# Hybrid encoder layer: one settle a round for VectorE's search tiles, all gates ahead of attention, low parts of the attention keys and values on GpSimd

## The chip, the core and the metric

The kernel runs on one core of a Trainium2 chip. The time is that of one execution on the device, in microseconds; a run gives one such time. Several engines work side by side, each through its own instructions in the order in which they were written to its queue: TensorE (PE; its weight loads are listed as PEld), VectorE (DVE), ScalarE (ACT), GpSimd (POOL) and SyncE (SP), which issues the DMA transfers.

## What is computed

One encoder layer over T = 1088 tokens (1024 of the prompt, 64 of a sample) with 1024 features: half a SwiGLU step, then a mixer, then half a SwiGLU step. Cut to the mixer, which the change touches:

```python
u = _rms(h, mix_norm)
q, k, v, qi, ki, wi, conv_in, gate = jnp.split(u @ w_in, points, axis=-1)   # after rotary: q, k, qi, ki
# sparse attention: each query keeps the top 256 admissible keys by an indexer score
score = jnp.einsum('bqh,bqhs->bqs', wi, jax.nn.relu(jnp.einsum('bqhd,bsd->bqhs', qi, k_idx)))
_, sel = lax.top_k(jnp.where(admissible, score, -jnp.inf), top)
attn = softmax(q . k[sel] / 8) @ v[sel]                                       # 8 heads, 2 key/value heads
# convolution branch
dc = depthwise_conv(concat(past_conv, ca * sigmoid(cb)), conv_w) + conv_b     # 31 taps, 512 channels
conv_out = silu(_layernorm(dc)) @ conv_w_out
# merge
g_a, g_c = split(sigmoid(gate + b_gate))                                      # 2 x 1024 gate columns
h = h + (g_a * (attn @ attn_w_out) + g_c * conv_out) @ w_out
```

## The kernel before

Values are kept transposed, features on the 128 partitions and tokens along the row. Tokens go in three chunks (`CHUNKS`) of 362 to 364. A float32 product is made of three matmuls on high and low parts (`mm3`, L136 to L138): high times high, high times low, low times high. A high part is a rounded copy that ScalarE makes, a low part the difference, a subtraction on VectorE or GpSimd (`split`, L152 and L153; for weights `wload`: DMA into `raw` at L117, `whi` on ScalarE at L118, `wlo` on GpSimd at L119).

The program around the change runs in these stages, of the profiled execution's 2411.5 us: the first SwiGLU to about 760 us, then the input projections and the indexer's scores, and then, from about 1060 us on, several kinds of work side by side:

- **The search** for the 256th best score of each query. Seven query tiles (named 5, 4, 3, 2, 1, 0, 6, with 1024, 896, 768, 640, 512, 384 and 192 keys) are searched by halving: each score is cut into a high and a low half of 16 bits; 15 rounds on the high halves (`search(15, …)`), `low_half` to prepare the low ones, 16 rounds on the low halves (`search(16, …)`). One round of one tile is a count of the keys at or above the candidate threshold (`count`; L907 on VectorE, L904 on ScalarE) and a settling, which moves the candidate up or down: on VectorE three small instructions for a group of tiles at once (`settle`, L914, L916, L918), on ScalarE two for each tile (`settle_x`, L925, L926). ScalarE has tile 5 in the 15-bit half and tiles 5 and 4 in the 16-bit half; VectorE has the rest in two groups, and the second group's counts stand between the first group's settling instructions.
- **The masks** (L964 to L984) that VectorE makes of the thresholds when the search is over, six instructions per tile, `bias` being the result.
- **The gates** (`gates`): 16 blocks of 128 gate columns, each 72 matmuls (three chunks of 24), evicted by ScalarE's tanh (`sg`, L1005) and stored to DRAM (`d_g`, L1006). `GPRE` = 14 blocks run ahead of attention, the last two as the first steps of the background.
- **The convolution**: for 60 rounds ScalarE makes `pd` (L679) and GpSimd adds it (L680).
- **The keys and values for attention** (`K`, `vt`), loaded and split while the search runs.

Then **attention** over nine query tiles in the order `TORD`, four pairs of heads each. `soft` makes a pair's logits (`lg`, matmuls L1052 and L1053) and VectorE adds the mask and takes the maximum (`pr`, `mb`, L1055); then ScalarE's exponential; `turn` transposes the probabilities (`pt`, L1079) and splits them into `ph` and `pl`; `values` multiplies them with `vt` into `pv`, which is evicted to `oh` and stored to `d_at`. Three pairs of logits run ahead of the pair that is being turned. After each slot of a pair, `fill` takes FILL[tile] steps of a **background** generator: the last gates, layer norm of the convolution (`norm`; `lx` loaded, `ls` added at L1141), its output product (`conv_out`), and for a chunk whose tiles are done `merge` (the stored attention is read back as `ar`, split into `ah` and `al`, multiplied, and gated by `ga`) and `wout`. After attention come the last merge and the second SwiGLU.

The order within each engine's queue comes from a scheduling of the whole program when it is built, in which the search and the masks have a high priority (`THI`); on the chip each engine keeps that order. The memory of the layer norm's pool (`ln`) is free only when the gates have read the activations `u`.

## Time and profile before

| | |
|---|---|
| median of 3 runs | 2418.17 us (2414.04 to 2422.6) |
| the profiled execution | 2413.27 us, its span 2411.5 us |
| mean granted TensorE clock | 0.987 |
| busy: PE, DVE, ACT, POOL | 96%, 73%, 50%, 58% of the span |
| DMA | 273.47 MB, 113 GB/s on average |

The span is what the profiler saw from the first to the last instruction. The busy share is an average over all stages; the change touches the stretch from about 1060 us to 1660 us, where the engines' shares are different from it. The granted clock is the share of full speed that TensorE was given, 1.0 being 2.4 GHz and 0.5 being 1.2 GHz.

### The profile page before, as it was taken

The numbers are of one execution on the slowest core, as the hardware profiler recorded it, in microseconds if no ns is written. First come the engines' busy times: TensorE is split into PE (matmuls) and PEld (weight loads), VectorE is DVE, ScalarE is ACT, GpSimd is POOL, SyncE is SP. The second block draws the span as 40 slices with busy tenths as digits, with TensorE's granted clock in tenths as the row PEclk, the third lists the DMA queues.
The fourth block names the chain that finished last, engine by engine and source line by source line (L and its number), as shares of the span: only waits on it lengthen the run. The fifth ranks groups of instructions, "written<-read, shape, count | busy, mean of one in ns | idle before, by whom it ended". The sixth has DMA issues, their size and how long they took to land. (4 is left out here: it accounts for less than half of the span.)

```text
span 2411.5 us, 44609 instructions
## 1 busy us (share of the span) xinstructions
PE 2307.2 (96%) x16762; PEld 2274.9 (94%) x16762; DVE 1762.6 (73%) x4051; ACT 1208.3 (50%) x2365; POOL 1407.7 (58%) x866
## 2 busy tenths in 40 slices
PE   7999999999999999999978999899999999999998
PEld 6999999999999999999977889799999999999997
DVE  7766667666677387799998976758666668776666
ACT  6433445343446556867956555536434445334343
POOL 5455556555557786878733456448555556545554
PEclk9999999999999999999989999899999999999999
DMA  5332223222224334333222546563223322332223
GB/s 191 106 106 88 95 99 125 88 97 97 97 97 139 132 125 127 95 102 105 92 83 83 167 145 191 164 211 117 86 88 104 99 99 71 116 105 96 96 102 112
DMA packets 130409, 273.47 MB, mean 113 GB/s; under 512 B 17936, under 2 KB 77200, under 8 KB 130192
## 3 DMA queue, kind: packets, MB, share of 16 engines
q1 hardware_dynamic: 130192, 270.61, 33.7%
q8 instruction: 132, 2.16, 0.4%
q14 instruction: 85, 0.70, 0.1%
HBM read 231.87 MB, written 38.75 MB: 112 GB/s over the span
## 5 line engine op out<-in xcount | busy, mean ns | idle before, releaser
L119 POOL TENSOR_TENSOR wlo<-raw,whi 128x1024 fp32r<-128x1024 f32 (+1 forms) x187 | 438.0, 2347 | 372.0 <-ACT whi L118 368.2
L136 PE MATMUL ps<-x,wp 128*128 128x272 f32 x1760 | 506.3, 289 | 2.7 <-ACT wp L152 2.6
L138 PE MATMUL ps<-x,wp 128*128 128x272 f32 x1760 | 503.5, 290 | 1.6 <-DVE wp L153 1.0
L137 PE MATMUL ps<-x,wp 128*128 128x272 f32 x1760 | 505.0, 288 | 0.0
L136 PE MATMUL ps<-x,whi 128*128 128x272 f32 (+2 forms) x1544 | 482.9, 313 | 14.0 <-ACT sg L1005 7.3
L138 PE MATMUL ps<-x,wlo 128*128 128x272 f32 (+2 forms) x1544 | 481.3, 312 | 0.3 <-POOL wlo L119 0.3
L137 PE MATMUL ps<-x,whi 128*128 128x272 f32 (+2 forms) x1334 | 411.6, 309 | 0.9 <-POOL x L153 0.9
L136 PE MATMUL ps<-gh,whi 128*128 128x272 f32 x1408 | 400.1, 289 | 5.6 <-DVE spare L284 3.5
L137 PE MATMUL ps<-gl,whi 128*128 128x272 f32 x1408 | 405.2, 289 | 0.0
L138 PE MATMUL ps<-gh,wlo 128*128 128x272 f32 x1408 | 404.1, 289 | 0.0
L153 POOL TENSOR_TENSOR wlo<-raw,whi 128x1024 fp32r<-128x1024 f32 x88 | 220.1, 2502 | 260.4 <-ACT whi L152 252.7
L136 PEld LDWEIGHTS ps<-x,wp 128*128 128x128 f32 x1760 | 331.2, 188 | 3.5 <-ACT wp L152 3.5
L138 PEld LDWEIGHTS ps<-x,wp 128*128 128x128 f32 x1760 | 328.8, 188 | 3.3 <-DVE wp L153 2.7
L137 PEld LDWEIGHTS ps<-x,wp 128*128 128x128 f32 x1760 | 331.5, 188 | 0.0
L153 POOL TENSOR_TENSOR wp<-s,wp 128x512 fp32r<-128x512 f32 x176 | 255.9, 1454 | 100.5 <-ACT wp L152 100.5
L136 PEld LDWEIGHTS ps<-x,whi 128*128 128x128 f32 x1544 | 293.2, 190 | 16.9 <-ACT sg L1005 8.2
L428 DVE SCALAR_TENSOR_TENSOR h<-ps,h 128x272 f32<-128x272 f32 x384 | 164.7, 439 | 186.8 <-PE ps L138 186.1
L118 ACT ACTIVATE whi<-raw 128x1024 fp32r<-128x1024 f32 (+1 forms) x187 | 190.6, 1020 | 214.9 <-PE ps L137 105.1
L138 PEld LDWEIGHTS ps<-x,wlo 128*128 128x128 f32 x1544 | 292.8, 190 | 1.7 <-POOL wlo L119 0.6
L680 POOL TENSOR_TENSOR ac<-ac,pd 128x559 f32<-128x559 f32 x180 | 260.5, 1447 | 57.7 <-ACT pd L679 24.1
L136 PEld LDWEIGHTS ps<-gh,whi 128*128 128x128 f32 x1408 | 263.6, 189 | 6.9 <-DVE spare L284 4.0
L138 PEld LDWEIGHTS ps<-gh,wlo 128*128 128x128 f32 x1408 | 266.3, 189 | 0.0
(235 smaller groups left out, 5010.6 us busy)
## 6 DMA issues: line engine op xcount, KB each, us to landing
raw<-wf SPq DMA_DIRECT2D x337, 512.0 KB, 3.3
raw<-wf SPq DMA_DIRECT2D x32, 384.0 KB, 3.0
d_g<-sg SPq DMA_DIRECT2D x32, 181.0 KB, 1.9
d_h<-h SPq DMA_DIRECT2D x2, 2176.0 KB, 10.5
y<-t SPq DMA_DIRECT2D x32, 136.0 KB, 1.9
raw<-d_q SPq DMA_DIRECT2D x32, 128.0 KB, 3.0
raw<-d_qi SPq DMA_DIRECT2D x24, 128.0 KB, 3.0
d_g<-sg SPq DMA_DIRECT2D x16, 182.0 KB, 3.2
```

The costliest lines, as they stand in the source:

```text
L118: nc.scalar.activation(hi[:, :n], raw[:, :n], AF.Copy)
L119: self.weng.tensor_tensor(lo[:, :n], raw[:, :n], hi[:, :n], op=ALU.subtract)
L136: t.matmul(out, wh, xh, start=first, stop=False)
L137: t.matmul(out, wh, xl, start=False, stop=False)
L138: t.matmul(out, wl, xh, start=False, stop=last)
L153: (eng or nc.vector).tensor_tensor(lo, x, hi, op=ALU.subtract)
L428: nc.vector.scalar_tensor_tensor(x, p, 0.5, x, op0=ALU.mult, op1=ALU.add)
L680: nc.gpsimd.tensor_tensor(ac, ac, pd, op=ALU.add)
```

## The change

1. **Search.** VectorE's tiles are one group (`VT`): all counts of a round, then one settling of all (its first instruction stands behind the first count). In the 16-bit half ScalarE has tiles 5 and 2 in place of 5 and 4 (1024 and 640 keys in place of 1024 and 896), so VectorE counts tile 4 in every round and tile 2 only in the 15-bit half. The low results of VectorE's tiles lie in the PSUM tile `srch`, those of ScalarE's in `lobx`; the masks are made for VectorE's tiles first.
2. **Gates.** All 16 run ahead of attention, and the background begins with the layer norm.
3. **Low parts.** The low parts of the attention keys (`kl`, twice) and values (`vt`, twice) are subtracted on GpSimd in place of VectorE.
4. **Order of attention tiles.** Tile 6 comes before tile 7.

```diff
-TORD = (7, 6, 8, 5, 4, 3, 2, 1, 0)
+TORD = (6, 7, 8, 5, 4, 3, 2, 1, 0)
-GPRE = 14
...
-            def load_k(pool, r0, name, tmp=None):
+            def load_k(pool, r0, name, tmp=None, eng=None):
...
-                self.split(kh, kl, raw)
+                self.split(kh, kl, raw, eng)
...
-            COL = {n: c for c, n in enumerate((5, 4, 3, 1, 2, 0, 6))}
-            GROUPS = {15: ((5,), (4, 3, 1), (2, 0, 6)), 16: ((5, 4), (3, 1), (2, 0, 6))}
-
+            COL = {n: c for c, n in enumerate((5, 2, 4, 3, 1, 0, 6))}
+            SPLIT = {15: ((5,), (2, 4, 3, 1, 0, 6)), 16: ((5, 2), (4, 3, 1, 0, 6))}
...
-            thr, low_ = sb_[:, 0:NT], sb_[:, 16:16 + NT]
+            thr, low_, lob = (sb_[:, 16 * i:16 * i + NT] for i in range(3))
...
                 for b in range(bits - 1, -1, -1):
+                    half = 0.5 * (1 << b)
                     if next(xs, 0) is None and bits == 15:
                         low_half(XT)
-                    for n in GA:
+                    for i, n in enumerate(VT):
                         count(n, b)
-                        next(sb, None)
-                    for _ in sb:
-                        pass
-                    sa = settle(GA, b)
-                    for n in GB:
-                        count(n, b)
-                        next(sa)
-                    sb = settle(GB, b)
-                for _ in sb:
-                    pass
+                        if i == 0:
+                            nc.vector.tensor_scalar(low_[:, g], cand[:, g], -half, None, op0=ALU.add)
+                    nc.vector.tensor_tensor(flag[:, g], cnt[:, g], thr[:, g], op=ALU.is_ge)
+                    nc.vector.scalar_tensor_tensor((res if b == 0 else cand)[:, g], flag[:, g], 2 * half, low_[:, g],
+                                                   op0=ALU.mult, op1=ALU.add)
...
-            search(15, I16, hib)
-            for g in ((4,), (3, 1), (2, 0, 6)):
+            search(15, I16, hib, hib)
+            for g in ((2,), (4, 3, 1, 0, 6)):
                 low_half(g)
-            search(16, U16, lob)
-            for g in map(cols, GROUPS[16]):
+            search(16, U16, lob, lobx)
+            for lo, g in ((lob, cols(SPLIT[16][1])), (lobx, cols(SPLIT[16][0]))):
...
-            K = [load_k(ak, 32 + 32 * g, str(g)) for g in range(2)]
+            K = [load_k(ak, 32 + 32 * g, str(g), eng=nc.gpsimd) for g in range(2)]
...
-            self.split(vt[:, 0, 0:9, :], vt[:, 1, 0:9, :], raw[:, 0:9, :])
-            self.split(vt[:SMP, 0, 9, :], vt[:SMP, 1, 9, :], raw[:SMP, 9, :])
+            self.split(vt[:, 0, 0:9, :], vt[:, 1, 0:9, :], raw[:, 0:9, :], nc.gpsimd)
+            self.split(vt[:SMP, 0, 9, :], vt[:SMP, 1, 9, :], raw[:SMP, 9, :], nc.gpsimd)
...
-            run(gates(gorder[:GPRE], ep))
+            run(gates(gorder, ep))
...
-                yield from gates(gorder[GPRE:], ak)
```

The lines of the kernel after are some 18 smaller: the logits are L1034 and L1035 there (L1052 and L1053 before), the maximum L1037 (L1055), the norm's add L1123 (L1141), the three matmuls L135 to L137.

TensorE's order between the gates and the first transposes, before: three pairs of logits, and then the gate matmuls of the last two blocks (`ps<-x`), the first row being the last of the fourteenth block.

```order
L138 MATMUL ps<-x,wlo 128x362
L1052 MATMUL lg<-kh_13639,qt 128x512
L1053 MATMUL lg<-kl_13640,qt 128x512
L1052 MATMUL lg<-kh_13639,qt 128x512
L1053 MATMUL lg<-kl_13640,qt 128x512
L1052 MATMUL lg<-kh_13639,qt 128x512
L1053 MATMUL lg<-kl_13640,qt 128x512
L136 MATMUL ps<-x,whi 128x364
L137 MATMUL ps<-x,whi 128x364
L138 MATMUL ps<-x,wlo 128x364
```

The same place after, the first two rows being the end of the sixteenth block.

```order
L136 MATMUL ps<-u,whi 128x362
L137 MATMUL ps<-x,wlo 128x362
L1034 MATMUL lg<-kh_13538,qt 128x448
L1035 MATMUL lg<-kl_13539,qt 128x448
L1034 MATMUL lg<-kh_13538,qt 128x448
L1035 MATMUL lg<-kl_13539,qt 128x448
L1034 MATMUL lg<-kh_13538,qt 128x448
L1035 MATMUL lg<-kl_13539,qt 128x448
L165 MATMUL ps<-ones,ls 128x128 x8
L1034 MATMUL lg<-kh_13538,qt 128x448
```

The 144 matmuls of the last two blocks moved from behind the first logits to ahead of them, and the norm's first column sums (`ps<-ones,ls`) stand where gate matmuls stood.

VectorE's order at the end of the masks, before: the last two masks, then the first maxima.

```order
L984 SCALAR_TENSOR_TENSOR bias<-bias,H_11249 128x1024
L984 SCALAR_TENSOR_TENSOR bias<-bias,H_11249 128x896
L1055 ISA pr,mb<-lg,bias 128x512
L1055 ISA mb 128x1
L1055 ISA pr,mb<-lg,bias 128x512
L1055 ISA mb 128x1
```

The same place after.

```order
L966 SCALAR_TENSOR_TENSOR bias<-bias,H_11249 128x1024
L966 SCALAR_TENSOR_TENSOR bias<-bias,H_11249 128x640
L1123 TENSOR_TENSOR ls<-lx 128x784
L1037 ISA pr,mb<-lg,bias 128x448
L1037 ISA mb 128x1
L1037 ISA pr,mb<-lg,bias 128x448
L1037 ISA mb 128x1
```

The norm's add moved ahead of the first maximum; before, it stood behind twelve of them.

TensorE's order where the first merge begins, before: its `ah` and `al` products come in one piece, behind the values (`pv`) of the first pair of tile 4.

```order
L136 MATMUL pv<-ph,vt 64x256
L137 MATMUL pv<-pl,vt 64x256
L138 MATMUL pv<-ph,vt 64x256
L136 MATMUL ps<-ah,whi 128x362
L137 MATMUL ps<-al,whi 128x362
L138 MATMUL ps<-ah,wlo 128x362
```

After, from the third pair of tile 5 on:

```order
L1034 MATMUL lg<-kh_13538,qt 128x320
L1035 MATMUL lg<-kl_13539,qt 128x320
L135 MATMUL ps<-ah,whi 128x362 x2
L1034 MATMUL lg<-kh_13538,qt 128x320
L1035 MATMUL lg<-kl_13539,qt 128x320
L1034 MATMUL lg<-kh_13538,qt 128x320
L1035 MATMUL lg<-kl_13539,qt 128x320
L135 MATMUL pv<-ph,vt 64x256
```

The merge's matmuls moved forward by one tile and stand singly between the logits and values of that tile's pairs, each behind the return of a piece of the attention that was stored shortly before.

## Rows read from the trace of the kernel before

**Rows 1.** The page: the chain that ended last, share of the span by engine.
```profile
PE 38%; DVE 6%; DMA 2%; ACT 1%; issue 1%; POOL 0%; SPq 0%; DVEq 0%; ACTq 0%; POOLq 0%
```
**Rows 2.** Windows: length, then busy us of PE, PEld, DVE, ACT, POOL; PEclk, DMA share, GB/s.
```profile
1130.00:1140.00 10.00, 10.00 (x62) 10.00 (x61) 9.72 (x37) 6.56 (x13) 9.68 (x7) 1.00 0.34 111
...
1260.00:1270.00 10.00, 2.30 (x6) 2.02 (x7) 9.73 (x15) 1.51 (x2) 0.00 (x0) 0.50 0.05 19
```
**Rows 3.** Timeline of PE: start us, us, operation, [idle before, releaser].
```profile
1147.78 0.43 PE L136 MATMUL ps<-x,whi 128*128 128x362 f32 x1 [3.58 <-ACT sg L1005]
...
1164.31 0.43 PE L136 MATMUL ps<-x,whi 128*128 128x362 f32 x1 [2.80 <-ACT sg L1005]
...
1172.33 0.33 PE L136 MATMUL ps<-x,whi 128*128 128x362 f32 x1
...
1184.22 0.33 PE L136 MATMUL ps<-x,whi 128*128 128x362 f32 x1
...
1233.18 0.79 PE L1052 MATMUL lg<-kh,qt 128*128 128x512 f32 x1 [5.25 <-ACT sg L1005]
...
1267.70 0.79 PE L1052 MATMUL lg<-kh,qt 128*128 128x512 f32 x1 [12.28 <-DVE mb L1055]
```
**Rows 4.** Timeline of ACT in the search's 16-bit half.
```profile
1145.38 1.15 ACT L904 ACTIVATE bias<-H,cand 128x1024 bf16<-128x1024 uint16 x1 [7.44 <-DVE cand L888]
...
1160.89 1.04 ACT L904 ACTIVATE bias<-H,cand 128x896 bf16<-128x896 uint16 x1 [4.40 <-DVE srch L887]
...
1236.99 0.29 ACT L926 ACTIVATE lob<-flag,cand 128x1 f32<-128x1 f32 x1
```
**Rows 5.** Timeline of DVE in the search: end of one round, and late in the 16-bit half.
```profile
1129.30 1.15 DVE L907 TENSOR_SCALAR_CACHE_REDUCE bias<-H,cand 128x896 bf16<-128x896 int16 x1
...
1134.15 0.14 DVE L916 TENSOR_TENSOR flag<-cnt,srch 128x3 f32<-128x3 f32 x1
...
1134.52 1.15 DVE L907 TENSOR_SCALAR_CACHE_REDUCE bias<-H,cand 128x896 bf16<-128x896 int16 x1
...
1225.45 0.88 DVE L907 TENSOR_SCALAR_CACHE_REDUCE bias<-H,cand 128x640 bf16<-128x640 uint16 x1
...
1232.09 0.16 DVE L918 SCALAR_TENSOR_TENSOR lob<-flag,srch 128x3 f32<-128x3 f32 x1
```
**Rows 6.** Timeline of DVE: low parts of keys and values.
```profile
1068.55 1.41 DVE L153 TENSOR_TENSOR kl<-raw,kh 128x1216 fp32r<-128x1216 f32 x1
...
1088.61 1.36 DVE L153 TENSOR_TENSOR vt<-raw,vt 128x1152 fp32r<-128x1152 f32 x1
```
**Rows 7.** Timeline of DVE: casts in the masks, and the first maximum.
```profile
1235.32 0.16 DVE L966 CAST mi<-lob 128x3 int32<-128x3 f32 x1
...
1251.79 2.37 DVE L966 CAST mi<-lob 128x2 int32<-128x2 f32 x1
...
1266.94 0.69 DVE L1055 CUSTOM_DVE_ANT_0 pr<-lg,bias 128x512 f32<-128x512 f32 x1 [0.24 <-issue]
```
**Rows 8.** Chain of waits: start us, us, engine and operation, at the norm.
```profile
1278.07 5.02 DMA lx<-d_dc
1283.11 0.98 DVE ls L1141
```
**Rows 9.** Timeline of POOL: low parts of weights.
```profile
1249.80 4.34 POOL L119 TENSOR_TENSOR wlo<-raw,whi 128x1024 fp32r<-128x1024 f32 x1 [14.68 <-ACT whi L118]
...
1280.18 2.40 POOL L119 TENSOR_TENSOR wlo<-raw,whi 128x1024 fp32r<-128x1024 f32 x1
```
**Rows 10.** Chain of waits: the return of a piece of attention to the merge.
```profile
1417.96 2.05 DMA d_at<-oh
1420.07 2.46 DMA ar<-d_at
1422.55 0.52 ACT ah L152
1423.09 2.63 DVE al L153
```

More of the change, by code (lines that the diff above doesn't have):

```diff
@@ L757, in run @@
             hib = kp.tile([P, NT], F32, name="hib")
-            lob = kp.tile([P, NT], F32, name="lob")
+            lobx = kp.tile([P, NT], F32, name="lobx")
             flag = kp.tile([P, NT], F32, name="flag")
@@ L888, in low_half @@
                 nc.vector.memset(cand[:, cg], float(1 << 15) - 0.5)
-                if g[0] in GROUPS[16][0]:
+                if g[0] in SPLIT[16][0]:
                     start_x(cg)
@@ L893, in start_x, with search @@
                 nc.vector.scalar_tensor_tensor(thx[:, cg], thr[:, cg], 2.0, lkx[:, cg], op0=ALU.mult, op1=ALU.add)
-            def search(bits, dt, res):
-                XT, GA, GB = GROUPS[bits]
+            def search(bits, dt, res, resx):
+                XT, VT = SPLIT[bits]
+                g = cols(VT)
                 def count(n, b):
@@ L908, in count @@
                                                 accum_out=cnt[:rows, c:c + 1])
-                def settle(t, b):
-                    g = cols(t)
-                    half = 0.5 * (1 << b)
-                    nc.vector.tensor_scalar(low_[:, g], cand[:, g], -half, None, op0=ALU.add)
-                    yield
-                    nc.vector.tensor_tensor(flag[:, g], cnt[:, g], thr[:, g], op=ALU.is_ge)
-                    yield
-                    nc.vector.scalar_tensor_tensor((res if b == 0 else cand)[:, g], flag[:, g], 2 * half, low_[:, g],
-                                                   op0=ALU.mult, op1=ALU.add)
-                    yield
                 def settle_x(n, b):
@@ L925, in settle_x @@
                     nc.scalar.activation(flag[:, c], cnt[:, c], AF.Sign, bias=thx[:, c])
-                    nc.scalar.activation((res if b == 0 else cand)[:, c], flag[:, c], AF.Identity,
+                    nc.scalar.activation((resx if b == 0 else cand)[:, c], flag[:, c], AF.Identity,
                                          bias=cand[:, c], scale=-0.5 * (1 << b))
@@ L936, in xrounds @@
                     yield
-                sb = iter(())
                 xs = xrounds()
@@ L942, in search @@
                 for b in range(bits - 1, -1, -1):
+                    half = 0.5 * (1 << b)
                     if next(xs, 0) is None and bits == 15:
                         low_half(XT)
-                    for n in GA:
+                    for i, n in enumerate(VT):
                         count(n, b)
-                        next(sb, None)
-                    for _ in sb:
-                        pass
-                    sa = settle(GA, b)
-                    for n in GB:
-                        count(n, b)
-                        next(sa)
-                    sb = settle(GB, b)
-                for _ in sb:
-                    pass
+                        if i == 0:
[3 more added lines that the diff above has]
+                                                   op0=ALU.mult, op1=ALU.add)
             nc.vector.memset(cand, float(1 << 14) - 0.5)
-            start_x(cols(GROUPS[15][0]))
-            search(15, I16, hib)
-            for g in ((4,), (3, 1), (2, 0, 6)):
+            start_x(cols(SPLIT[15][0]))
+            search(15, I16, hib, hib)
+            for g in ((2,), (4, 3, 1, 0, 6)):
                 low_half(g)
-            search(16, U16, lob)
-            for g in map(cols, GROUPS[16]):
+            search(16, U16, lob, lobx)
+            for lo, g in ((lob, cols(SPLIT[16][1])), (lobx, cols(SPLIT[16][0]))):
                 nc.vector.tensor_copy(mi[:, 0, g], hib[:, g])
-                nc.vector.tensor_copy(mi[:, 1, g], lob[:, g])
+                nc.vector.tensor_copy(mi[:, 1, g], lo[:, g])
                 nc.vector.tensor_scalar(mi[:, 0, g], mi[:, 0, g], 16, None, op0=ALU.logical_shift_left)
```

## The prediction

> **What bounds the kernel now.** I read the page's chain first: TensorE carries 38% of the span on it by its own matmuls and VectorE 6%, the other engines 2% or less each [rows 1]. So an edit gains only where TensorE stands idle. The windows between 1060 and 1660 us, where all edits lie, show where that is: at 1130 to 1140 TensorE is busy for the whole window, at 1260 to 1270 for 2.30 of 10 us while VectorE is busy for 9.73 [rows 2]. TensorE's timeline gives the waits. The longest is 12.28 us before 1267.70, a logit matmul that needs its PSUM buffer back from the first maximum, and VectorE reaches that maximum only at 1266.94, when the last mask is done [rows 3, 7]. One of 5.25 us ends at 1233.18, where the first logits wait for ScalarE's last gate eviction, and two of 3.58 and 2.80 us stand among the gates for the same reason [rows 3]. ScalarE itself stood still for 7.44 and 4.40 us just ahead of these two, until VectorE had prepared the low halves of its tiles [rows 4]. VectorE is thus the head of the queue at both places: search, masks, first maximum.
>
> **Search.** A settling's last two instructions take from 1134.15 to 1134.52, that is 0.37 us in which VectorE counts nothing, and they follow a count's sum at once [rows 5]. The first instruction of the three runs under a count and is not charged. Two settlings a round become one: 31 rounds × 0.37 = 11.5 us less. Against that VectorE now counts tile 4 (896 keys, 1.15 us) where it counted tile 2 (640 keys, 0.88) in 16 rounds [rows 5]: 16 × 0.27 = 4.3 us more. That the settling of all tiles now stands directly ahead of a count which needs its result could add a latency that the order before hid. The flag, which needs the sum just made, comes without a gap [rows 5], so I take nothing for it; 31 × 0.1 = 3 us is the upper bound I keep, a quarter of the settling itself. ScalarE's second tile shrinks by as much as VectorE's grows, so ScalarE keeps to its pace; its last result came at 1236.99, and it is needed only when VectorE's five masks are done [rows 4]. Before, the masks of ScalarE's tiles began at 1251.79 [rows 7].
>
> **Low parts.** The keys' two subtractions cost VectorE 1.41 us each and the values' 1.36 [rows 6]: 4.2 us less while the search runs (the small fourth is left out). GpSimd takes them instead. For 1024 elements it needs 2.40 us [rows 9], so for 1216, 1216 and 1152 some 2.85 + 2.85 + 2.70, and about 0.4 for the small one: 8.8 us between its additions for the convolution. ScalarE's conv products wait for these through two buffers, and its gate evictions queue behind them in order. This is what could hold TensorE up at the gates; with 1.0 granted and 10 us busy at 1130 to 1140, beside a GpSimd busy for 9.68, it doesn't do so yet [rows 2]. Bounds: 0 and 8.8 us on the gates' end; I take 0, as TensorE is the later engine in that row.
>
> The search thus ends 11.5 − 4.3 + 4.2 = 11.4 us earlier, at 1232.25 − 11.4 = 1220.9 [rows 5]. The masks are the same seven tiles; they took from 1232.25 to 1266.70 (0.24 ahead of the first maximum at 1266.94 [rows 7]), 34.4 us, and end at 1255.3.
>
> In the masks one cast of 2 elements took 2.37 us where another took 0.16, and in the same time a weight's low part took GpSimd 4.34 us where another took 2.40 [rows 7, 9]: the two engines held each other up by about 2 us. The Trainium skill has the rule for this, SBUF — State Buffer, section "SBUF: two separate sides": GpSimd and VectorE share a pair of ports, locked for a whole instruction by whichever starts first, when VectorE's instruction is in a two-port mode or reads two SBUF inputs, and the other "fully blocks". That speaks against this change, which puts more subtractions on GpSimd beside VectorE's search. The trace agrees at that cast, and the counts of the search, at 1.15 us beside an almost full GpSimd [rows 2, 5], show nothing of it.
>
> **Gates and the norm.** The 5.25 us wait goes: the fifteenth gate's matmuls follow the fourteenth's at 1227.93 (1233.18 − 5.25) [rows 3]. A gate of 72 matmuls takes 1184.22 − 1172.33 = 11.89 us [rows 3], two take 23.8, to 1251.7. Of the 6.4 us of waits among the gates I take half as gone, since VectorE prepares the low halves earlier (15 of the 31 settlings and the 4.2 us lie ahead of it): 1248.5, with 1245.3 and 1260.5 (all waits gone; none gone and GpSimd's 8.8 on top) as bounds. Now the added wait. The norm's add stands ahead of the first maximum in VectorE's order; it needs `lx`, whose load took 5.02 us [rows 8] and can start only when the last gate matmul has read `u`. So `lx` lands at 1248.5 + 0.2 + 5.0 = 1253.7, 1.6 us before VectorE is through with the masks, and costs only its own 0.98 us [rows 8]. The first maximum comes at 1255.3 + 1.0 = **1256.3, 10.6 us earlier**. Queued behind that add are the maxima, and TensorE behind these, so every us that `lx` is later than 1255.3 is a us of all. TensorE is done with gates and three pairs of logits at about 1251 and waits some 5 us instead of 12.28. Its clock stood at 0.50 in the old wait [rows 2]; I count no gain from it, as it will fall in the new one too.
>
> **Behind the first maximum.** TensorE then has 32 gate matmuls less to do, those that stood interleaved with the fourth pair of logits: 32 × 0.165 = 5.3 us. Some of that filled time in which it would have waited. Against it, the last two gates are no longer there as filling, the background runs six steps ahead, and tiles 5 and 4 have less beside them. The first merge moved ahead into the pairs of tile 5, and each of its four pieces needs a store, a load, and two splits, 2.05 + 2.46 + 0.52 + 2.63 = 7.7 us [rows 10], between the pair that makes it and the matmuls that read it. I take 1 us of waiting a piece, 4 in all (bounds 0 and 7.7 each), and let it stand against the 5.3. The order of tiles 6 and 7 gives nothing: one has 448 and the other 512 keys a piece, and both come first.
>
> **Sum.** 2413.27 − 10.6 = 2402.7 on the profiled execution. The median of the runs is 4.9 above it, by a factor of 1.0020: **2407.5 us**.
>
> **Rivals.** *The merge in tile 5 waits (slower).* TensorE keeps its order, so a piece that isn't back stops the logits behind it as well. If each of the four costs its whole 7.7 us, that is 31 us instead of 4: −10.6 − 5.3 + 31 = +15, 2433. It decides from (10.6 + 5.3) / 4 = 4.0 us a piece on, where nothing is gained, and shows a loss by over 7 us from 5.8 on. For it speaks that piece and reader are only a pair or so apart, against it that a pair's logits, transposes and values stand between.
>
> *The gates end late (same).* If GpSimd's 8.8 us pass through ScalarE to TensorE, the gates end at 1257 to 1260, `lx` lands at 1262 to 1265, and the first maximum is at 1263 to 1266, up to 4 us earlier than now: 2415 to 2418, I say 2416. For it: the same stretch already has waits on ScalarE [rows 3]. Against it: their cause there was VectorE's low halves [rows 4].
>
> *The port lock (same).* If each of GpSimd's new subtractions stopped VectorE for its length, 8.8 us come back on the search and the first maximum is at 1265.1: a gain of 1.8, 2416. The cast row is for it, the counts beside a busy GpSimd against it [rows 2, 5, 7]. The page named above would have it so where a count uses both ports.
>
> *All waits are regained (more).* If the 12.28 and the 5.25 us vanish, as the 5.3 us of matmuls moved and the shorter search together allow at most, 17.5 to 19 are gained: 2399. It would need TensorE to find other work while the masks finish, and its order shows logits only.
>
> **How the numbers follow.** Forecast 0.45; all regained 0.15; gates late 0.22; port lock 0.08; merge waits 0.10. A measurement of this kernel can tell about 0.3% from no change, 7.3 us. Faster by more: 0.45 + 0.15 = 0.60; same 0.22 + 0.08 = 0.30; slower 0.10. The range runs from 2399 to 2419: the forecast with its bounds, the fuller gain at the low end, the two cases of no change at the high end with the spread of the runs; the merge's waits, and half of the fuller gain, lie outside.
>
> **What would show it.** In the profile after, in this order: the search's rounds shorter by 0.37 us in the 15-bit half and by 0.1 (0.37 − 0.27) in the other; TensorE's wait of 5.25 us gone and the last gate matmul near 1248; `lx` landing before the last mask; the first maximum near 1256; TensorE's wait there 4 to 7 us; and waits of TensorE for `ah` or `al` in tile 5 of about a us. The forecast is wrong if `lx` is what VectorE's add waits for, if a round's settling is longer than 0.37 us, or if the merge's waits in tile 5 add up to more than 10 us.

## The result: slower by 0.7%, and the profile after

The kernel after takes 2433.62 us (median of 6 runs, 2428.82 to 2440.64), the kernel before 2417.95 us in the runs beside it: a ratio of 1.0068, with a 95% interval from 1.0048 to 1.0089. A gain of 0.4% was forecast. The time is that of the rival in which the merge waits in tile 5, 2433 us, but its mechanism accounts for little of it (below).

In the profiled execution the span is 2429.0 us against 2411.5. From the first count of the search, 1061.74 us, to the end of the last values it takes 511.4 us; before it took 498.8, counted in the same way. These 12.6 us are what there is to explain. They lie inside the interval of the ratio (11.6 to 21.5 us). The rest of the 17.5 us between the two spans is not the change's: 0.7 us stand ahead of the search, and some 4 us come about behind the last values, where one wide addition of VectorE takes 6.62 us in place of 2.78; it also takes 6.7 us in kernels that are as fast as before or faster (last section).

The chain of the page has the same shape as in [rows 1]:

```profile
PE 36%; DVE 6%; DMA 3%; ACT 1%; issue 1%; POOL 1%; SPq 0%; DVEq 0%; ACTq 0%; POOLq 0%
```

Windows of the kernel after (length, then busy time of TensorE, its loads, VectorE, ScalarE, GpSimd, granted clock, DMA share, GB/s), the stretch that [rows 2] shows of before:

```profile
1260.00:1270.00 10.00, 0.00 (x0) 0.00 (x0) 10.00 (x14) 0.01 (x1) 0.00 (x0) 0.58 0.81 290
```

TensorE's timeline there, to be read beside the last two of [rows 3]:

```profile
1257.98 0.47 PE L1034 MATMUL lg<-kh,qt 128*128 128x448 f32 x1 [1.44 <-ACT sg L987]
...
1270.77 3.79 PE L165 MATMUL ps<-ones,ls 128*128 128x128 f32 x16 [11.31 <-DVE ls L1123]
```

The wait of 5.25 us ahead of the first logits has become 1.44; it was forecast to go. The wait of 12.28 us is still there with 11.31, only behind another instruction: it ends with the norm's add, and VectorE's timeline shows why this came so late.

```profile
1269.76 0.96 DVE L1123 TENSOR_TENSOR ls<-lx 128x784 f32<-128x784 f32 x1
1270.64 0.61 DVE L1037 CUSTOM_DVE_ANT_0 pr<-lg,bias 128x448 f32<-128x448 f32 x1
```

The add waits for nothing, it follows the last mask. The first maximum is at 1270.64, 208.9 us after the first count; before it took 205.9. So 3.0 of the 12.6 us are lost up to the first maximum, where 10.6 were to be gained, and 9.6 between the first maximum and the last values: 302.5 us against 292.9.

**The first round of the search.** VectorE's timeline after, and under it the same instructions before; then GpSimd's after.

```profile
1065.48 3.66 DVE L805 TENSOR_SCALAR Y<-Y,sgn 128x512 f32<-128x512 f32 x3
...
1069.14 2.06 DVE L806 COPY H<-Y 128x512 int16<-128x512 int16 x3
1071.13 2.36 DVE L801 TENSOR_TENSOR thr<-thr,ktop 128x7 f32<-128x7 f32 x1
```
```profile
1064.79 1.02 DVE L807 TENSOR_SCALAR Y<-Y,sgn 128x512 f32<-128x512 f32 x3
...
1065.82 0.84 DVE L808 COPY H<-Y 128x512 int16<-128x512 int16 x3
1066.60 1.37 DVE L803 TENSOR_TENSOR thr<-thr,ktop 128x7 f32<-128x7 f32 x1
```
```profile
1066.19 2.84 POOL L152 TENSOR_TENSOR kl<-raw,kh 128x1216 fp32r<-128x1216 f32 x1 [0.65 <-ACT kh L151]
1068.99 2.10 POOL L679 TENSOR_TENSOR ac<-ac,pd 128x559 f32<-128x559 f32 x1
1071.05 2.42 POOL L118 TENSOR_TENSOR wlo<-raw,whi 128x1024 fp32r<-128x1024 f32 x1
```

A subtraction of 1216 elements that VectorE no longer does stands on GpSimd from 1066.19 to 1069.03, and in about that time three VectorE instructions, of 1.02 us together before, take 3.66. The addition of 7 elements at 1071.13 takes as long as the weights' subtraction beside it. The three VectorE groups take 4.85 us more than before, so that the first round gives back more than the 4.2 us that the move saved. In e1 below, without that subtraction on GpSimd, they take 3.25 us in all, as before (3.23).

**The masks.** VectorE and GpSimd after:

```profile
1228.59 1.23 DVE L950 TENSOR_TENSOR mth<-mi 128x5 int32<-128x5 int32 x1
1229.86 1.32 DVE L951 TENSOR_TENSOR sth<-mth,sgn 128x5 f32<-128x5 f32 x1
...
1254.22 2.37 DVE L948 CAST mi<-lobx 128x2 int32<-128x2 f32 x1
...
1256.90 3.37 DVE L961 TENSOR_SCALAR H<-Y,mth 128x1024 bf16<-128x1024 f32 x2
```
```profile
1227.39 2.42 POOL L118 TENSOR_TENSOR wlo<-raw,whi 128x1024 fp32r<-128x1024 f32 x1 [0.81 <-ACT whi L117]
1229.75 6.24 POOL L679 TENSOR_TENSOR ac<-ac,pd 128x559 f32<-128x559 f32 x3
...
1245.60 10.98 POOL L118 TENSOR_TENSOR wlo<-raw,whi 128x1024 fp32r<-128x1024 f32 x1 [5.44 <-ACT whi L117]
```

GpSimd's last three additions for the convolution, which before ended at 1220.06, now stand at 1229.75 to 1235.99, in the masks. Instructions of 5 columns take 1.23 and 1.32 us beside them and the weights' subtraction ahead of them. From the last count to the last mask it is 41.9 us, where before it was 35.3. Not all of this comes of the low parts: the subtraction that stands from 1245.60 on and the one that follows it are of weights for the gates, and beside them a cast of 2 columns takes 2.37 us and two comparisons 3.37. In e3 below, with two gates fewer ahead of attention, the same instructions are short. VectorE's timeline of e3:

```profile
1255.61 0.16 DVE L949 CAST mi<-lobx 128x2 int32<-128x2 f32 x1
...
1256.08 1.21 DVE L962 TENSOR_SCALAR H<-Y,mth 128x1024 bf16<-128x1024 f32 x2
```

The masks take 37.3 us in e3 and 37.3 in e1, which has the low parts back on VectorE, and 33.0 in e4, which has neither part. So the low parts and the gates hold the masks up by some 4.6 us each; the prediction priced neither in the masks.

### The profile page after: what moved, and what is told of

The parts are those of the page before. It is cut to its first block, busy times and chain, and to the rows that moved or that the text cites. A ratio compares the mean times of both kernels' runs of the same rounds, so it can differ in the third digit from the quotient of the medians.

```text
span 2429.0 us, 44521 instructions
## 1 busy us (share of the span) xinstructions
PE 2319.2 (95%) x16762; PEld 2284.7 (94%) x16762; DVE 1771.7 (73%) x3946; ACT 1205.2 (50%) x2365; POOL 1424.6 (59%) x870
## 5 line engine op out<-in xcount | busy, mean ns | idle before, releaser
L118 POOL TENSOR_TENSOR wlo<-raw,whi 128x1024 fp32r<-128x1024 f32 (+1 forms) x187 | 446.1, 2390 | 379.0 <-ACT whi L117 374.1
L135 PE MATMUL ps<-x,wp 128*128 128x272 f32 x1760 | 507.2, 290 | 3.9 <-ACT wp L151 3.8
L137 PE MATMUL ps<-x,wp 128*128 128x272 f32 x1760 | 504.4, 290 | 1.6 <-DVE wp L152 1.0
L135 PE MATMUL ps<-x,whi 128*128 128x272 f32 (+2 forms) x1544 | 484.2, 314 | 16.7 <-ACT sg L987 8.0
L137 PE MATMUL ps<-x,wlo 128*128 128x272 f32 (+2 forms) x1544 | 481.8, 313 | 0.0
L135 PE MATMUL ps<-gh,whi 128*128 128x272 f32 x1408 | 400.1, 289 | 5.6 <-DVE spare L283 3.5
L137 PE MATMUL ps<-gh,wlo 128*128 128x272 f32 x1408 | 404.1, 289 | 0.0
L135 PEld LDWEIGHTS ps<-x,wp 128*128 128x128 f32 x1760 | 331.9, 189 | 5.2 <-ACT wp L151 5.2
L137 PEld LDWEIGHTS ps<-x,wp 128*128 128x128 f32 x1760 | 329.6, 189 | 3.5 <-DVE wp L152 2.7
L135 PEld LDWEIGHTS ps<-x,whi 128*128 128x128 f32 x1544 | 293.8, 190 | 19.4 <-ACT sg L987 8.9
L137 PEld LDWEIGHTS ps<-x,wlo 128*128 128x128 f32 x1544 | 293.8, 190 | 0.9
L135 PEld LDWEIGHTS ps<-gh,whi 128*128 128x128 f32 x1408 | 263.5, 189 | 6.9 <-DVE spare L283 3.9
L137 PEld LDWEIGHTS ps<-gh,wlo 128*128 128x128 f32 x1408 | 266.2, 189 | 0.0
```

Source lines behind the costliest of these rows:

```text
L118: self.weng.tensor_tensor(lo[:, :n], raw[:, :n], hi[:, :n], op=ALU.subtract)
L135: t.matmul(out, wh, xh, start=first, stop=False)
L137: t.matmul(out, wl, xh, start=False, stop=last)
```

## The experiments

Theories at the start: that GpSimd's additional work holds VectorE up (port lock); that attention has become longer for want of the gates as filling, or because of the merge; and against these that the masks are longer because of their grouping. Later, the theory that the order which the build's scheduling finds for attention decides (theory A).

The table holds all twelve. "Rows" is how far TensorE's order is from that of the kernel before: its 16,762 matmuls in the trace were compared line by line, and the lines that differ counted on both sides, so that a matmul that moved counts twice. (The expectations count rows of a shorter listing, 16,507, and have 505, 38 and 46 for f4, g2 and g3.) The times in the next two columns are read from one profile each: first count of the search to first maximum, first maximum to the end of the last values. How far such a reading varies is seen from g1, whose order is that of before: some 2 us. The ratios are to before's runs beside each, and need not be the quotient of two medians. "Waits" is what TensorE's logits wait for VectorE's maxima from 13 us after the first maximum to the last values.

| kernel | rows | count to maximum | maximum to values | waits | median us | ratio to before (95%) |
|---|---|---|---|---|---|---|
| before | 0 | 205.9 | 292.9 | 0.6 | 2417.95 to 2420.61 | 1 |
| after | 984 | 208.9 | 302.5 | 4.6 | 2433.62 | 1.0068 (1.0048 to 1.0089) |
| e1, keys back | 984 | 204.9 | 302.5 | 5.1 | 2430.94 | 1.0052 (1.0039 to 1.0066) |
| e2, fewer taps | 984 | 206.8 | 304.2 | 5.3 | 2431.25 | 1.0051 (1.0036 to 1.0066) |
| e3, 14 gates | 694 | 205.5 | 310.5 | 4.6 | 2438.41 | 1.0088 (1.0073 to 1.0104) |
| e4, search only | 548 | 200.1 | 306.2 | 4.8 | 2425.81 | 1.0028 (1.0016 to 1.0041) |
| f1, tiles 6 and 7 | 754 | 206.7 | 303.7 | 4.7 | 2431.14 | 1.0051 (1.0034 to 1.0069) |
| f2, 16 gates | 1052 | 209.0 | 303.8 | 8.3 | 2432.43 | 1.0055 (1.0038 to 1.0073) |
| f3, low parts | 662 | 209.1 | 302.9 | 6.3 | 2432.83 | 1.0059 (1.0044 to 1.0074) |
| f4, one settle | 626 | 197.9 | 303.5 | 6.8 | 2421.52 | 1.0011 (1.0001 to 1.0021) |
| g1, order of counts | 0 | 206.5 | 295.0 | 2.3 | 2421.64 | 1.0 (0.9988 to 1.0011) |
| g2, one settle, 15 gates | 38 | 197.9 | 292.9 | 0.9 | 2411.99 | 0.9956 (0.994 to 0.9971) |
| g3, 15 gates | 44 | 206.6 | 291.9 | 2.0 | 2421.52 | 0.9997 (0.9984 to 1.0011) |
| g4, written order | 1126 | 195.6 | 366.7 | 4.6 | 2483.29 | 1.0264 (1.0248 to 1.028) |

Attention's window doesn't hold the same work in all of them. Before has 1786 matmuls in it; f1, f3, f4, g1, g2 and g3 have 1782 to 1791, and after, e1, e2 and f2 have 1754, the gates being done. But e3 has 1830, e4 1817 and g4 1898; what they have more than before are gate matmuls not yet done at the first maximum, by the 0.165 us that one takes in [rows 3] about 7, 5 and 18 us of their times. e1 and e2 have after's order of TensorE without a difference, and take 302.5 and 304.2 us of attention where after takes 302.5.

### e1: low parts back on VectorE

```diff
-            K = [load_k(ak, 32 + 32 * g, str(g), eng=nc.gpsimd) for g in range(2)]
+            K = [load_k(ak, 32 + 32 * g, str(g)) for g in range(2)]
...
-            self.split(vt[:, 0, 0:9, :], vt[:, 1, 0:9, :], raw[:, 0:9, :], nc.gpsimd)
+            self.split(vt[:, 0, 0:9, :], vt[:, 1, 0:9, :], raw[:, 0:9, :])
```

> The kernel after, with the low parts of the attention keys and values back on VectorE. Theory of the port lock: GpSimd's 8.8 us are gone from the convolution's way, so its last addition comes some 9 us earlier (1236.0 to about 1227), ahead of the masks. The 4.8 us that VectorE lost in the search's first round and the 4.5 us that it lost to additions in the masks go, the 4.2 us of the subtractions come back: first maximum at about 1265.5 instead of 1270.6, time about 2428. Rival (the masks are longer because of how the tiles are grouped, not because of GpSimd): the masks stay at 41 us and the first maximum comes 4 us later, about 2438. Rival (the loss lies in attention alone): first maximum moves, time stays within 2 us of 2433.6.

The first maximum came 204.9 us after the first count, 4.0 earlier than in the kernel after (5 were expected), although VectorE does 4.2 us of subtractions more. The masks take 37.3 us. VectorE's timeline of e1 at their start, GpSimd's convolution being over at 1221.57:

```profile
1233.39 0.17 DVE L950 TENSOR_TENSOR mth<-mi 128x5 int32<-128x5 int32 x1
1233.59 0.17 DVE L951 TENSOR_TENSOR sth<-mth,sgn 128x5 f32<-128x5 f32 x1
```

0.17 us in place of 1.23 and 1.32: what made them long was GpSimd beside them, not the grouping. The median fell by 2.7 us, to 2430.94, and not to 2428; that is less than runs of one kernel differ by (after: 2428.82 to 2440.64). Attention's 302.5 us did not move. So the lock shows in the profile, and most of the loss is elsewhere.

### e2: fewer additions on GpSimd

```diff
-                        nc.gpsimd.tensor_tensor(ac, ac, pd, op=ALU.add)
+                        if not (t == 2 and s0 == 559 and j > 30 - 12):
+                            nc.gpsimd.tensor_tensor(ac, ac, pd, op=ALU.add)
```

> The kernel after, without the last 12 of GpSimd's 180 additions of the convolution (ScalarE still makes their products, so the convolution's last half tile is not complete). Nothing else is changed. Theory of the port lock: GpSimd is done with the convolution 17 us earlier, at about 1219, ahead of the masks; these shrink from 41.4 us to about 37 (the two locks by weight splits, 2.2 us each, stay), and the first maximum comes 4.5 us earlier; the search's first round keeps its 4.8 us. Time about 2429. Rival (grouping): the masks stay at 41 us and the time at 2433.

This kernel leaves out 12 additions, so the convolution's last half tile lacks these terms. The masks are 37.5 us, as the lock has it. The first maximum came 2.1 us earlier and not 4.5, as the search itself was 2.3 us longer in this profile (168.5 against 166.2 us from first to last count). 2431.25 us, 2.4 less than after, and within its runs' spread as well.

### e3: 14 gates

```diff
+GPRE = 14
...
-            run(gates(gorder, ep))
+            run(gates(gorder[:GPRE], ep))
...
+                yield from gates(gorder[GPRE:], ak)
```

> The kernel after, with 14 gates ahead of attention and two in the background as before. Theory (the last gates were filling that attention now lacks): from the first transposes to the end of tile 4, TensorE's waits fall from 20.7 us back to about 14, and the time to about 2425; the first maximum still comes at about 1270. Rival (the merge moved into tile 5 is what costs): it moves back with the gates, and its waits for the merge's pieces, 1.5 us in the kernel after, cannot give back more than that: 2432. Rival (gates ahead of attention gain, as forecast): 2440 or more.

A miss: 2438.41, slower than after. Attention with the gates back takes 310.5 us, not less. It has 76 gate matmuls more than after, some 13 us by [rows 3], and is 8.0 us longer, so in part they did fill waits. The first maximum came 3.4 us earlier, as the masks are 37.3 us. The times alone would say that moving the gates gained 4.8 us.

### e4: the new search alone

The kernel before with part 1 of the change, as in its diff:

```diff
...
-            GROUPS = {15: ((5,), (4, 3, 1), (2, 0, 6)), 16: ((5, 4), (3, 1), (2, 0, 6))}
...
+            SPLIT = {15: ((5,), (2, 4, 3, 1, 0, 6)), 16: ((5, 2), (4, 3, 1, 0, 6))}
...
```

> The kernel before with the new search alone (one settle a round, ScalarE's second tile 2). From the rounds of the kernel after (4.91 and 4.10 us against 5.22 and 4.15): the search ends 15 x 0.31 + 16 x 0.05 = 5.5 us earlier. Theory of the port lock: GpSimd's convolution still ends at about 1220, 7 us ahead of the masks, so the masks keep to 34 to 35 us and the first maximum comes 5 us earlier than before's 1266.9; time about 2413 against 2418. Rival (grouping lengthens the masks): masks 39 to 41 us, nothing gained, 2418 or more.

The first maximum came 5.8 us earlier than before, as expected, and the masks are 33.0 us, so grouping lengthens nothing. The time still rose to 2425.81 instead of falling to 2413: attention takes 306.2 us, 13.3 more, of which about 5 are its 31 gate matmuls more. Nothing in attention was edited here.

### f1: only the order of two attention tiles

```diff
-TORD = (7, 6, 8, 5, 4, 3, 2, 1, 0)
+TORD = (6, 7, 8, 5, 4, 3, 2, 1, 0)
```

> The kernel before with attention's tiles 6 and 7 in the other order; no instruction is added or taken away, but the program's scheduling gives TensorE another order all through attention. Theory A (attention's time hangs on the order that the scheduling happens to give, and before's order is a good one): first maximum as before near 1267, from there to the last values 5 to 10 us longer than before's 293, time 2424 to 2428 against 2419. Theory B (only where the search, the gates and the low parts are matters): within 2 us of before.

Theory A, and by more than it said. No instruction is added or taken away, and the first maximum comes 206.7 us after the first count, as before. Attention takes 303.7 us, 10.8 more, and the kernel 2431.14. What the two tiles' exchange does by itself is not told apart here from the order that comes with it.

### f2: only the gates

```diff
-            run(gates(gorder[:GPRE], ep))
+            run(gates(gorder, ep))
...
-                yield from gates(gorder[GPRE:], ak)
```

> The kernel before with all 16 gates ahead of attention and nothing else. From the kernel after against its variant with 14 gates (2433.6 and 2438.4): 4.8 us gained, 2415 against before's 2419. Rival (filling that attention lacks): 2424 or more, with TensorE's waits between first transposes and the end of tile 4 at 20 us instead of 14.

2432.43: alone, the gates' move costs 12 us, where e3 against after had it gain 4.8. The time is the rival's. Lost filling is not needed for such a loss, as f1, f3 and f4 have before's gates in attention and lose as much of it, and in g3 below one gate fewer stands there at no cost. But for two gates with before's order otherwise there is no run, so what share of it is the filling stays open, here and in the kernel after. Effects of the four parts cannot be added or taken from each other: f1, f2, f3 and the search cost 10.5, 11.8, 12.2 and some 6 us one by one, and 15.7 together.

### f3: only the low parts

The kernel before with part 3 of the change:

```diff
...
-            K = [load_k(ak, 32 + 32 * g, str(g)) for g in range(2)]
+            K = [load_k(ak, 32 + 32 * g, str(g), eng=nc.gpsimd) for g in range(2)]
...
-            self.split(vt[:, 0, 0:9, :], vt[:, 1, 0:9, :], raw[:, 0:9, :])
+            self.split(vt[:, 0, 0:9, :], vt[:, 1, 0:9, :], raw[:, 0:9, :], nc.gpsimd)
```

> The kernel before with the low parts of keys and values on GpSimd and nothing else. Theory of the port lock: VectorE's first round of the search is some 4 us longer, the convolution ends near 1230 to 1236 instead of 1220 and overlaps the first masks, which grow from 34 to 37 to 39 us; 4.2 us of subtractions are saved: first maximum 1269 to 1272, time 2422 to 2426. Rival (what GpSimd does beside VectorE costs nothing): first maximum 4 us earlier, 1263, time 2415.

The first maximum comes 3.2 us later than before, as the lock has it, and the convolution ends at 1237.53. The masks, though, are 35.9 us and not 37 to 39; what was lost is in the search (173.0 us from first to last count against 170.4). The time of 2432.83 is above what the lock accounts for; attention takes 302.9 us.

### f4: one settle, ScalarE's tiles as before

The new search of e4 with the old tiles on ScalarE:

```diff
...
-            SPLIT = {15: ((5,), (2, 4, 3, 1, 0, 6)), 16: ((5, 2), (4, 3, 1, 0, 6))}
+            SPLIT = {15: ((5,), (4, 3, 1, 2, 0, 6)), 16: ((5, 4), (3, 1, 2, 0, 6))}
...
```

> The kernel before with one settle a round and ScalarE's tiles 5 and 4 as before. VectorE's rounds become 4.91 and about 3.83 us: the search is 15 x 0.31 + 16 x 0.32 = 9.8 us shorter and the first maximum comes at about 1257. Theory A (attention's order): what the first maximum gains is given back in attention as with the new search alone (there 6 us gained and 13 lost), 2420 to 2425. Theory C (the exchange of tile 4 for tile 2 is what lost): 2410.

The first maximum comes 8.0 us earlier than before (9.8 were expected), and attention, with 2 matmuls more, gives it back: 303.5 us, 10.6 more; 2421.52 us, theory A.

### g1, g2, g3: edits that leave attention's order

g1 turns the order of three counts round, which the scheduling answers with no other order of TensorE at all.

```diff
-                    for n in GA:
+                    for n in GA[::-1]:
                         count(n, b)
```

> The kernel before with the three counts of VectorE's first group in the other order within each round. The work is the same and so is the order of TensorE, ScalarE and GpSimd. Theory A (attention's time hangs on the order that the scheduling gives): as before, 2417 to 2423; from first maximum to last values 293 us, TensorE's logits wait for maxima less than 1 us in all. Rival (before's profile was a lucky execution, and its attention takes 300 us as a rule): 300 us or more, with waits for maxima of 4 us.

g2 is f4 with one gate more ahead of attention:

```diff
-GPRE = 14
+GPRE = 15
```

> The kernel before with one settle a round (ScalarE's tiles 5 and 4 kept) and 15 gates ahead of attention. The 15th gate makes up for the shorter search in the scheduling's eyes: TensorE's order differs from before's in 38 rows of 16,507, where that with one settle and 14 gates differs in 505. Theory A: first maximum near 1258 as with 14 gates, and now attention keeps before's 293 to 295 us: 2410 to 2413. Rival (the gain of an earlier first maximum is lost in attention whatever the order is): 2420 or more, attention 300 us or more.

g3 is the kernel before with the same edit.

> The kernel before with 15 gates ahead of attention. TensorE's order differs from before's in 46 rows, VectorE's in 2: the 72 matmuls move ahead of the first logits, and nothing behind. Theory A: the same work stands ahead of the first maximum, which VectorE sets: 2418 to 2421, attention 293 us. Rival (a gate ahead of attention costs half of what two cost, 12 us): 2426.

All three came out by theory A, but for g1's waits for maxima, 2.3 us where less than 1 was expected. g1 and g3 measure as before (1.0 and 0.9997) with 295.0 and 291.9 us of attention. g2 has f4's first maximum, 197.9 us after the first count, and before's attention of 292.9 us: 2411.99 us, **faster than both kernels** by the interval (0.994 to 0.9971). f4 and g2 differ by one gate's place, and by 9.5 us. That gate gains nothing by itself, since g3 has it with before's search and measures as before. VectorE's order behind the first maximum goes with TensorE's, 356 differing rows in f4 and 2 in g2, so which of the two engines' orders costs the time is not told apart.

What TensorE waited for in attention, from some 15 us behind the first maximum on (line waited at, line waited for, us in total, times, longest), first before, then f4, then g2:

```profile
PE pt L1079 <- DVE pl L153: 6.7, 6, 1.9
PE ps L136 <- DVE ga L1215: 4.9, 2, 3.4
...
PE ps L166 <- DVE ls L1141: 2.0, 1, 2.0
...
PE lg L1052 <- DVE mb L1055: 0.6, 2, 0.4
```
```profile
PE lg L1035 <- DVE mb L1038: 6.8, 7, 1.9
PE ps L136 <- DVE ga L1198: 6.1, 3, 3.4
PE ps L166 <- DVE ls L1124: 3.6, 2, 2.2
PE pt L1062 <- DVE pl L153: 2.5, 7, 1.0
```
```profile
PE pt L1062 <- DVE pl L153: 7.2, 9, 2.0
PE ps L136 <- DVE ga L1198: 5.7, 3, 3.3
PE ps L166 <- DVE ls L1124: 2.0, 1, 2.0
...
PE lg L1035 <- DVE mb L1038: 0.9, 2, 0.7
```

Where the order is far from before's, TensorE waits longer at its logits for VectorE's maxima, and what stands behind them in its order waits too. The kernel after has 4.6 us of it:

```profile
PE ps L135 <- DVE ga L1197: 9.2, 3, 4.1
PE pt L1061 <- DVE pl L152: 5.0, 6, 1.1
PE lg L1034 <- DVE mb L1037: 4.6, 4, 3.4
...
PE ps L135 <- ACT ah L151: 1.4, 3, 0.6
...
PE ps L136 <- POOL al L152: 0.7, 2, 0.5
```

The waits of after come to 28.2 us in all against 21.0. The waits for `ga`, the merge's gating, have grown by as much as those for the maxima, from 4.9 to 9.2 us, and the new one stands in the first merge, the one that moved ahead. TensorE's row and VectorE's in after:

```profile
1466.05 0.43 PE L135 MATMUL ps<-ah,whi 128*128 128x362 f32 x1 [3.49 <-DVE ga L1197]
```
```profile
1465.46 0.53 DVE L1197 SCALAR_TENSOR_TENSOR ga<-ga,ps 128x362 f32<-128x362 f32 x1 [2.61 <-DMA ga<-d_g]
```

VectorE itself waits there for the gate's values to be read back from DRAM. The other part is the clock: windows over attention as a whole, before, after and g2, have a granted clock of 0.97, 0.95 and 0.97.

```profile
1267.00:1560.00 293.00, 269.75 (x1786) 251.78 (x1786) 231.69 (x606) 170.37 (x370) 143.64 (x76) 0.97 0.47 145
```
```profile
1271.00:1573.00 302.00, 271.72 (x1754) 251.84 (x1754) 232.17 (x604) 166.42 (x366) 143.50 (x75) 0.95 0.43 130
```
```profile
1262.00:1555.00 293.00, 269.29 (x1783) 250.13 (x1783) 229.44 (x604) 170.22 (x370) 143.70 (x76) 0.97 0.48 145
```

The kernel after has 32 matmuls of the gates less to do in its window, 5.3 us by [rows 3], and yet TensorE is busy in it for 2.0 us longer: more of its matmuls ran at 1.2 GHz. Idle it is for 7.0 us longer (30.3 against 23.3). In all, TensorE had the lower clock for 18.8 us of before's attention, 16.3 of g2's and 31.9 of after's. In after the clock fell at 1350.37, 1394.74, 1466.42 and 1558.58, each time within or just behind a wait of TensorE of 1.5 to 4.1 us, so a wait there seems to cost more than its length.

### g4: the order of the text

```diff
-MS = lambda nc: set()
+MS = lambda nc: {nc.tensor.engine}
```

> The kernel before with one settle a round, 14 gates, and TensorE kept to the order of the program's text all through attention, in place of the order that the scheduling finds (with this, an edit of the search no longer moves anything of TensorE's in attention). Theory A says only that the order matters, not that this one is good. If logits that stand ahead of VectorE's maxima are what costs, their waits are below 2 us here, since the text puts each piece of logits behind the transposes of a slot, attention takes 293 to 297 us, and the time is 2412 to 2416. If the scheduling's order is worth more than that, attention takes 300 us or more as with one settle and 14 gates, 2421 or more.

A miss, and a large one: 2483.29 us. Attention takes 366.7 us, with these longest waits:

```profile
PE pt L1062 <- POOL pr L1052: 27.3, 15, 7.0
PE pv L136 <- ACT oh L1088: 11.0, 5, 4.8
PE pt L1062 <- DVE pl L153: 7.9, 7, 4.1
```

The first maximum (195.6 us after the first count) is as early as in g2. Against f4, the same kernel in the order that the scheduling finds, it is 62 us: so much can an order alone cost here. About 18 us of attention are the 112 gate matmuls that the written order leaves behind the first maximum. The logits' waits, 4.6 us, are the smaller part, so they are a sign of a worse order and not the only way in which one loses.

## Why the prediction was wrong

The sum had 10.6 us to gain up to the first maximum and nothing to lose behind it. In the profile 3.0 are lost up to the first maximum and 9.6 behind it. So two parts of it failed: up to the first maximum 13.6 us were missed, some 7 in the search and some 7 in the masks, which the sum kept at 34.4 us; behind it 9.6.

- **Behind the first maximum.** The step of this name takes 32 matmuls less and 4 us of waits for the merge, sets them against each other, and lets the rest of attention stand as it was. The order of all of attention had moved (984 rows), and attention takes 9.6 us more in the profile, with 5.3 us less work in it. That such a move by itself costs as much is shown by f4 and g2; for the kernel after it is inferred, as no run has its parts with before's order. The sentence "The order of tiles 6 and 7 gives nothing" is wrong in the same way: it looked at the work of the two tiles, and f1 measures 10.5 us for their exchange and the order that comes with it. The working looked at where the scheduling had moved the rows that a term rested on and gave every other moved row a price of nothing.
- **Search.** 11.4 us earlier was forecast; from first to last count it is 166.2 us instead of 170.4, 4.2 less. Settles: a 15-bit round fell from 5.22 to 4.91 us and a 16-bit one from 4.15 to 4.10, 0.05 to 0.06 less each than the sum had. VectorE's rows at a round's end after, and under them two of a round's end before:

```profile
1220.18 1.15 DVE L906 TENSOR_SCALAR_CACHE_REDUCE bias<-H,cand 128x896 bf16<-128x896 uint16 x1
...
1223.79 0.07 DVE L906 DVE_READ_ACCUMULATOR bias<-H,cand 64x1 f32 x1
1223.90 0.16 DVE L936 TENSOR_TENSOR flag<-cnt,srch 128x5 f32<-128x5 f32 x1
1224.09 0.16 DVE L937 SCALAR_TENSOR_TENSOR cand<-flag,srch 128x5 f32<-128x5 f32 x1
1224.29 1.15 DVE L906 TENSOR_SCALAR_CACHE_REDUCE bias<-H,cand 128x896 bf16<-128x896 uint16 x1
```
```profile
1227.18 0.08 DVE L907 DVE_READ_ACCUMULATOR bias<-H,cand 64x1 f32 x1
1227.18 0.14 DVE L916 TENSOR_TENSOR flag<-cnt,srch 128x2 f32<-128x2 f32 x1
```

  The flag starts 0.11 us after the last sum's read began, where before it starts with it. The prediction took the latter for a flag that needs the sum just made. It is not: before, the flag behind the three tiles' counts has 2 columns, those of the other group, whose sums were long there. So [rows 5] could not show what a flag costs directly behind its own sum. A settling now takes 0.50 us from that read to the next count, longer than 0.37, which is one of the signs of being wrong that the prediction named. Over 31 rounds the difference to the sum is 1.7 us, inside the bound of 3 that the prediction kept. The larger part of the 7.2 us missed is the first round's 4.85 us.
- **Low parts and the port lock.** The lock was a rival at 0.08, at 8.8 us, on the ground that counts run at 1.15 us beside a full GpSimd. That holds after too (the row at 1224.29 above). But the search and the masks are not only counts: copies, multiplications by a column and instructions with two inputs were held, by 4.85 us in the first round and, with the low parts on GpSimd, by some 4.6 in the masks (41.9 us against e1's 37.3). The rows that the prediction had (a cast of 2.37 us instead of 0.16) were of these kinds; the step that failed is taking the counts for all of VectorE's work. The Trainium skill's SBUF — State Buffer, section "SBUF: two separate sides", says that the loser of the shared ports "fully blocks" for the whole instruction. The trace agrees: VectorE's 7 columns took 2.36 us beside a subtraction of 2.42. In the other direction it shows more than one instruction's length: GpSimd's subtraction took 10.98 us instead of 2.40 through a whole run of VectorE's instructions in the masks. What the lock costs in the time is not resolved: e1 and e2 are 2.7 and 2.4 us below after, less than its runs differ by.
- **GpSimd's end.** The 8.8 us were counted against TensorE's gates only, where I took them at nothing. With them the convolution's last addition moved from 1220.06 to 1235.99, out of the search and into the masks; in e1 it is at 1221.57. That the masks had been clear of it was a cover which the prediction did not name, and the term that held the masks at 34.4 us failed by it, and by as much again for the gates' weights, whose low parts GpSimd makes there too.
- **Gates and the norm.** Right: of the 5.25 us wait 1.44 is left, and the norm's add waited for nothing. Wrong in size: the waits among the gates did not halve (8.0 us against 7.3), and the last eviction of a gate ended at 1257.93, where the gates' end was forecast for 1248.5. It cost nothing, as VectorE was later still. The rival in which the gates end late thus had the gates' time right, 1257 to 1260, and `lx`'s, which landed 6.2 us after its issue at 1257.97. But nothing waited for it, and GpSimd's low parts are not shown to be the cause: in e1, without them, the last eviction ends at 1257.95.
- **The rival that gave 2433.** Its time was hit by luck: TensorE's waits for `ah` and `al` in all of attention come to 1.4 + 0.7 = 2.1 us in the rows above, against 31. The merge that moved ahead did cost a wait of 3.49 us, but for `ga`, which no term named. A time that agrees doesn't prove the case it was worked out for.
- **The sum** was made against one execution of before, 4.9 us below the median. Some 4 us of this are in one instruction of VectorE (last section).

**What stays open**: which of the moved rows cost attention its 10 us, apart from the 3.49 us for `ga`, and whether an order as good as before's exists for the new tile split, the 16 gates and the low parts on GpSimd. No run has one of these with fewer than 548 differing rows. Only the end points are shown: thirteen kernels with the scheduled order, of which the nine with 548 or more differing rows take 302 to 311 us of attention (302 to 304 without e3 and e4, whose windows hold more gate matmuls), and the four with 44 or fewer, before among them, 292 to 295.

## What to carry to other kernels

Where a scheduler orders the program at build time, compare the whole order of the engine that bounds it before pricing an edit. An edit that moves hundreds of rows far from its place is a new draw of the order, worth some 10 us here, as much as the whole gain that was forecast. Such a move can be made up for elsewhere (one gate more ahead) so that the order stays, and only then is the edit measured for itself. Single-part experiments that each re-draw the order can't be added up; a pair with nearly the same work in two orders (f4 and g2) and a control with other code in the same order (g1) tell the two apart. And before work is moved to GpSimd, look at which VectorE instructions stand beside it and beside all that it pushes back, by their kind and not by the busiest kind.

## What the runs showed of the hardware that was not expected

- A VectorE addition of 7 columns took 2.36 us, and an OR of 5 columns 1.23 us, beside GpSimd's subtractions; in e1 the OR took 0.17.
- GpSimd's subtraction of 1024 columns took 10.98 us in one place of the masks, and 11.24 in e1, where most took 2.38 to 2.42.
- In the second SwiGLU's weights one VectorE addition of 512 columns with two inputs, 2.78 us in the profile of before, took 6.6 to 6.7 us in the kernel after and in all twelve runs. From the last values to the end it is 851.7 us in the profile of before, and 853.4 to 857.1 in these. As g1 and g3 have before's work there, before's profiled execution was probably some 4 us luckier than usual. VectorE's timeline of g2:

```profile
1643.51 6.70 DVE L308 TENSOR_TENSOR ps<-raw 128x512 f32<-128x512 f32 x1
```
